# Keys of a sample group transposed in 32x32 blocks on VectorE, scores in 32x32 tiles of TensorE

## The chip, the cores and the metric

One core of one Trainium2 chip runs the whole program. The metric is the device time of one execution in microseconds; a kernel's time is the median of three runs. Times inside a profile are microseconds from the start of the profiled execution's span.

## The reference, cut to what matters

The program is one inference step of a two-layer decoder trunk, over 1024 prompt tokens and a sample group of 8 sequences with 8 new tokens each. The change touches the differential attention of the first layer, for the sample group: each sequence has 512 past keys in a paged cache (4 pages of 128 tokens, found by a page table), 8 heads, and two query/key components (c) of 64 channels per head, so a key of one token is 1024 numbers.

```python
q = rms_norm(zq.reshape(b, l, H_A, 2, DH_A), q_g) * (DH_A ** -0.5)
k = rms_norm(zk.reshape(b, l, H_A, 2, DH_A), k_g)
...
k_past = cache_k[j, page_table].reshape(db, past_len, H_A, 2, DH_A)
v_past = cache_v[j, page_table].reshape(db, past_len, H_A, DV_A)
k_all = jnp.concatenate([k_past, k], axis=1)
...
s = jnp.einsum('bqhcd,bkhcd->bhcqk', q, k)
s = s + bias                       # by the distance, the same for both components
s = jnp.where(causal, s, -jnp.inf)
p = jax.nn.softmax(s, axis=-1)
a = p[:, :, 0] - lam * p[:, :, 1]
return jnp.einsum('bhqk,bkhe->bqhe', a, v)
```

A sample has 8 heads x 2 components x 8 queries = 128 rows of scores over 512 past and 8 new keys. Everything here is float32.

## The kernel before

The program goes through stages: a projection of queries, keys and values with the attention of the prompt (to about 586 us), the stage of the sample group (about 586 to 832 us), and then the gated MLP, the output projection and the second layer. The change lies in the sample stage, with a little preparation ahead of it.

**The sample stage** walks over 32 pages, four for each of the 8 samples. Its loop over steps s (from L638 on) calls, in each step, the parts below with a lag of so many pages behind the page that is loaded. That table of lags, LAG = (10, 7, 5, 3) for out_t, av_s, att_t and soft, sets a rough order; a scheduler that orders the program when it is built then places each instruction on its engine's queue, and each engine takes its queue strictly in that order.

- pages (L517 to L522): a raw key page kp, 128 tokens x 1024 channels, 512 KB, is loaded on SP's queue. There are two kp buffers.
- vpages (L524 to L529): the same for a value page vp, six buffers, on SP as well.
- key_trans (L531 to L540): for each half of a page (hh = 0: heads 0 to 3, hh = 1: heads 4 to 7), TensorE transposes four 128x128 blocks into one PSUM bank (ktp, two banks, L539), and VectorE (hh = 0) or ScalarE (hh = 1) copies it into the transposed keys kT of that half (L540). There are three kT buffers, two to a sample.
- soft (L542 to L564): the scores ssc of a sample. The queries lie in qbd, for each head block-diagonal over its two components, with the rows of the other half zero. For each half and each of four column tiles of 32 columns there is one matmul with 128 channels and 512 past keys, and one with the 8 new keys (L550). VectorE then adds the bias to the last columns (L555), takes the maximum (snm, L558), ScalarE takes the exponential with its sum (spp, L560), and VectorE makes the reciprocal with its sign (sss, L561 and L562) and scales a combination matrix with it (cmb, L564).
- att_t (L567 to L577): matmuls with cmb transpose the probabilities and subtract the second component (an L571, ap L575), copied to sat by VectorE and ScalarE.
- av_s (L579 to L594): attention times values, sop (L586): four column tiles x four value pages and the new values; then squares on ScalarE (ssq), a norm on POOL, and son on VectorE (L593).
- out_t (L597 on): son is transposed (sot) and scaled to the output.

**The filling.** Between these steps the loop calls 52 units of projection work, about 4.8 to a sample, in a fixed order: first the rest of the gate units (gate_a, L242 to L259, PSUM name ga, 24 matmuls of up to 384 columns), then 36 units of the MLP's value branch (vb_unit, PSUM name zv, 24 matmuls of 256 columns). All take their accumulator from one PSUM name with two banks. A zv unit ends in a copy zs (L623), on VectorE for even and ScalarE for odd units, and a store on SP (L624).

**Ahead of the stage**, the prompt loop normalizes the sample rows' queries and keys and transposes them on TensorE per head (qk_trans with i == NT - 1), into qbd and ksT, and bias_sample loads the bias in 16 small DMAs.

## Time and profile before

| | |
|---|---|
| time, median of three runs | 1801.37 us (1799.54 to 1802.87) |
| span of the profiled execution (the page gives no other time of it) | 1806.1 us |
| TensorE: matmuls / weight loads | 1747.1 us (97%) / 1629.0 us (90%) |
| VectorE | 1012.4 us (56%) |
| ScalarE | 755.4 us (42%) |
| GpSimd (POOL) | 609.3 us (34%) |
| moved by DMA | 211.62 MB, mean 117 GB/s |

In the rows below PE is TensorE's matmuls, PEld its weight loads, DVE VectorE, ACT ScalarE, POOL GpSimd, SP SyncE, which only issues transfers (SPq). L12 is line 12 of the kernel. A busy share is an average over stages that have different limits, so a stage is read by stretches: how much of them an engine is busy, and, where it idles, which instruction or transfer ended the wait. "idle before <-X" is that time and what ended it. PEclk is the granted clock of TensorE as a share of full speed.

### The profile page before, as it was taken

The page shows a single profiled execution, that of the slowest core. Times are in us where ns is not written, and L with a number is a line of the kernel's source. Part 1 is how long each engine was busy: PE and PEld are TensorE (multiplying, and loading weights), DVE is VectorE, ACT ScalarE, POOL GpSimd, SP SyncE. Part 2 cuts the span into 40 slices and gives each one's busy share as a digit, 9 for nine tenths or more (in the row PEclk, how much of TensorE's full clock was granted, in tenths as well). Part 3 has the DMA queues.
Part 4 walks back from the last instruction along what each step waited for, and adds up shares of the span by engine and source line. Part 5 has one row for each costly group of instructions (what it writes and reads, how often), then busy time and mean ns, then how long its engine had stood idle before and what let it go on. Part 6 is the DMA issues. An engine that isn't in the chain of part 4 may idle for free.

```text
span 1806.1 us, 31855 instructions
## 1 busy us (share of the span) xinstructions
PE 1747.1 (97%) x11429; PEld 1629.0 (90%) x11429; DVE 1012.4 (56%) x2223; ACT 755.4 (42%) x1934; POOL 609.3 (34%) x893
## 2 busy tenths in 40 slices
PE   7999999999999899999899999999999999998999
PEld 6798999999999888889899999999999999996777
DVE  5898888988983233223832342444354455667442
ACT  4566656666664222223222232333343334345241
POOL 4555646655653221112721200044111232235230
PEclk8999999999999999999999999999999999999999
DMA  7102202211213766746221262432334244438741
GB/s 211 52 23 73 68 20 67 67 43 43 66 59 104 243 202 232 236 165 213 59 79 54 92 199 74 129 97 82 94 116 152 80 126 123 130 111 260 240 130 71
DMA packets 223302, 211.62 MB, mean 117 GB/s; under 512 B 22286, under 2 KB 201143, under 8 KB 223143
## 3 DMA queue, kind: packets, MB, share of 16 engines
q1 hardware_dynamic: 203510, 194.35, 34.7%
q10 hardware_dynamic: 19632, 15.21, 2.8%
q8 instruction: 91, 1.49, 0.4%
q14 instruction: 69, 0.56, 0.1%
HBM read 151.35 MB, written 56.24 MB: 115 GB/s over the span
## 4 chain that ended last, share of the span: by engine, by line
PE 62%; DVE 16%; DMA 9%; ACT 4%; POOL 4%; issue 4%; SPq 0%; ACTq 0%; POOLq 0%; DVEq 0%
PE o L1373 5%; PE yo L143 3%; PE yo L145 3%; PE yo L144 3%; PE vg L143 3%; PE vg L144 3%; PE vg L145 3%; DMA oT_d<-oTr 2%; DVE p L418 2%; PE zv L143 1%; PE zv L144 1%; PE zv L145 1%; PE o L434 1%; PE s L399 1%; PE qkv L143 1%
## 5 line engine op out<-in xcount | busy, mean ns | idle before, releaser
L412 ACT ACTIVATE p<-s,nm 128x256 f32<-128x256 f32 (+7 forms) x128 | 95.0, 747 | 38.3 <-DVE nm L409 22.3
L399 PE MATMUL s<-ks,qs 128*128 128x512 f32 (+3 forms) x384 | 96.5, 364 | 2.8 <-DVE ks L384 1.4
L87 ACT CAST qs<-qs 64x256 fp32r<-64x256 f32 x128 | 51.7, 404 | 76.8 <-DVE qs L381 74.2
L1120 POOL TENSOR_TENSOR e<-e,k 128x256 f32<-128x256 f32 (+1 forms) x50 | 42.4, 853 | 117.1 <-ACT e L1117 100.8
L338 POOL TENSOR_TENSOR sq<-qk 128x256 f32<-128x256 f32 (+1 forms) x72 | 46.9, 652 | 95.0 <-ACT qk L87 94.2
L434 PE MATMUL o<-v,at 128*128 128x128 f32 x576 | 76.8, 279 | 1.6 <-ACT at L87 1.6
L399 PEld LDWEIGHTS s<-ks,qs 128*128 128x128 f32 x384 | 64.9, 190 | 12.6 <-ACT p L412 2.8
L434 PEld LDWEIGHTS o<-v,at 128*128 128x128 f32 x576 | 71.4, 193 | 4.2 <-ACT at L87 2.6
L131 POOL TENSOR_TENSOR s<-s,mhalf 128x4 f32<-128x4 f32 (+1 forms) x72 | 73.3, 1018 | 5.3
L837 DVE TENSOR_TENSOR yp<-yp,yo 128x384 f32<-128x384 f32 (+1 forms) x48 | 25.3, 530 | 74.5 <-ACT yp L836 41.7
L407 DVE TENSOR_REDUCE nm<-s 128x1 f32<-128x640 f32 (+3 forms) x64 | 65.2, 1019 | 1.2
L747 POOL TENSOR_TENSOR u<-u,th 128x384 f32<-128x384 f32 (+1 forms) x24 | 28.7, 1194 | 99.9 <-DVE th L746 99.4
L405 DVE TENSOR_TENSOR s<-s,tb 128x256 f32<-128x256 f32 (+1 forms) x128 | 52.8, 412 | 8.9 <-PE s L399 5.6
L418 DVE SCALAR_TENSOR_TENSOR p<-p,fac,p 128x128 f32<-128x128 f32 (+3 forms) x64 | 55.1, 861 | 1.7
L1373 PE MATMUL o<-w1h,oh 128*128 128x512 f32 x128 | 53.0, 414 | 2.5 <-ACT oh L1350 2.5
L87 ACT COPY at<-atp 128x512 f32<-128x512 f32 (+2 forms) x96 | 44.5, 481 | 20.0 <-PE atp L427 19.8
L746 DVE SCALAR_TENSOR_TENSOR th<-th,gb 128x384 f32<-128x384 f32 (+1 forms) x24 | 12.6, 524 | 69.0 <-ACT th L745 69.0
L1373 PE MATMUL o<-w1l,oh 128*128 128x512 f32 x128 | 50.8, 397 | 0.0
L1373 PE MATMUL o<-w1h,ol 128*128 128x512 f32 x128 | 50.3, 407 | 0.0
L427 PE MATMUL atp<-cf,p 128*128 128x128 f32 x288 | 46.8, 275 | 1.9 <-DVE p L418 1.8
L343 POOL TENSOR_TENSOR qk<-qk,s 128x256 f32<-128x256 f32 (+1 forms) x72 | 46.6, 647 | 4.7
L381 DVE SCALAR_TENSOR_TENSOR qs<-qkt,qg,qs 64x128 fp32r<-64x128 f32 x128 | 44.5, 348 | 3.6
(825 smaller groups left out, 6340.4 us busy)
## 6 DMA issues: line engine op xcount, KB each, us to landing
kp<-in_cache_k SPq DMA_DIRECT2D x32, 512.0 KB
vp<-in_cache_v SPq DMA_DIRECT2D x32, 512.0 KB
or<-oT_d SPq DMA_DIRECT2D x16, 384.0 KB
vb_d<-zs SPq DMA_DIRECT2D x36, 128.0 KB
oT_d<-ob SPq DMA_DIRECT2D x8, 544.0 KB
gt<-g_d SPq DMA_DIRECT2D x34, 128.0 KB
xt<-in_x_prompt SPq DMA_DIRECT2D x8, 512.0 KB
out<-v ACTq DMA_DIRECT2D x64, 64.0 KB
```

Of the source, the lines that this page charges most:

```text
L87: act.activation(o, i_, AF.Copy, scale=scale) if scale is not None else act.copy(o, i_)
L131: pool.tensor_tensor(dst, dst, mhalf[:dst.shape[0], :n], ALU.pow)
L143: pe.matmul(out, lh, rh, start=(s == 0), stop=False)
L144: pe.matmul(out, lh, rl, start=False, stop=False)
L145: pe.matmul(out, ll, rh, start=False, stop=(s == n - 1))
L399: pe.matmul(sc[c][:, k0:k0 + w], qs[:, c, l], kts[h, j][:, c, :w], start=(l == 0), stop=(l == 1))
L405: dve.tensor_tensor(sc[c][:, lo:n], sc[c][:, lo:n], tb[:, h, 256 - (n - lo):], ALU.add)
L407: dve.tensor_reduce(nm[:, c:c + 1], sc[c][:, :n], axis=AX.X, op=ALU.max, negate=True)
L412: act.activation(pc[:, :n], sc[c][:, :n], AF.Exp, bias=nm[:, c:c + 1], accum_out=ss[:, c:c + 1])
L418: dve.scalar_tensor_tensor(pt[0][:, :n], pt[1][:, :n], fac, pt[0][:, :n], ALU.mult, ALU.add)
L434: pe.matmul(op[:, :P], at[:, j * P:(j + 1) * P], vts[h, j], start=(j == 0), stop=(j == i))
L1373: pe.matmul(it.mp[:r], lh[:, k, :r], rh[k][:, cs], start=(k == 0 and a == 0), stop=(k == KT - 1 and a == 2))
```

## The change

Queries and keys of the sample rows are no longer transposed on TensorE. Ahead of the stage, GpSimd multiplies the queries by the norm's weights (qgr), and queries and keys go to DRAM (qs_d, ks_d), two DMAs per head. The bias tile biasS gets the shape 128 x 4 x 34 and 32 small DMAs instead of 16. A mask qmask is added to the constants.

In the stage, the key order in the PSUM scores is by residue: of each page, tokens are cut into four groups a of 32, and each row group of TensorE works on one of them.

- key_trans: VectorE transposes each half page (128 x 512) in 32x32 blocks straight from kp into kT (now 128 x 16 x 130); neither TensorE nor PSUM takes part. GpSimd copies the sample's new keys (kn2, made once at the start of the stage) into the last two columns.
- q_rep (new, called behind key_trans of page 1 of each sample): one DMA of 512 KB brings the sample's 8 queries, 16 times over, into qx; GpSimd multiplies by the mask that leaves each row its own half and component; VectorE transposes 128 x 1024 in 32x32 blocks into qr, one buffer.
- soft: 128 matmuls with 32 channels, 32 columns of weights and 130 keys, each placed on one of the 16 tiles of 32x32 by tile_position, into four PSUM banks (in place of two, and the two of ktp). Bias and maximum go over the new shape; the exponential is cut in two, with two sums that VectorE adds.

The rest of the stage, its buffers (kp 2, vp 6, kT 3, two accumulator banks) and its lags are the same. The diff, cut to its core:

```diff
-        qbd = mid.tile([P, H, NB, 2, 2, 8], F32, name="qbd")
-        pool.memset(qbd, 0.0)
-        ksT = mid.tile([P, H, NS], F32, name="ksT")
         vsm = mid.tile([NS, H, P], F32, name="vsm")
-        biasS = mid.tile([P, 136], F32, name="biasS")
+        biasS = mid.tile([P, 4, 34], F32, name="biasS")
+        qgr = mid.tile([NS, P], F32, name="qgr")
+        qmask = mid.tile([P, 2 * H], F32, name="qmask")
...
-                nc.sync.dma_start(biasS[r0:r0 + 8, :], tb[0:8, h, 0:136])
+                nc.sync.dma_start(biasS[r0:r0 + 8, :, 0:32], tb[0:8, h, 0:128].rearrange("p (a k) -> p a k", a=4))
+                nc.sync.dma_start(biasS[r0:r0 + 8, :, 32:34], tb[0:8, h, 128:136].rearrange("p (a k) -> p a k", a=4))
...
+                if i == NT - 1:
+                    G[PRM['kg']].tensor_tensor(qk[:r, :128], qk[:r, :128], qgr, ALU.mult)
+                    nc.sync.dma_start(qs_d[:, h * P:(h + 1) * P], qk[:r, :128])
+                    nc.sync.dma_start(ks_d[:, h * P:(h + 1) * P], qk[:r, 128:])
+                    return None
...
-                if i == NT - 1:
-                    for c in range(2):
-                        q8 = slice(c * DH, (c + 1) * DH)
-                        act.activation(qbd[q8, h, :, h // 4, c, :], tp[q8, 0:NS].rearrange("p (b q) -> p b q", b=NB),
-                                       AF.Copy, scale=qg[q8])
-                    dve.tensor_copy(ksT[:, h, :], tp[:, 128:128 + NS])
-                    return None
...
+            kn = pb.tile([P, D], F32, tag="vn", name="kn", bufs=1)
+            dve.memset(kn, 0.0)
+            for a in range(4):
+                nc.sync.dma_start(kn[a * 32:a * 32 + 2 * NB, :],
+                                  ap_of(ks_d, 2 * a * D, [[8 * D, NB], [D, 2], [1, D]]))
+            knT = pb.tile([P, 32, 32], F32, tag="qx", name="knT", bufs=1)
+            dve.transpose(knT, kn.rearrange("p (j d) -> p j d", j=32))
+            kn2 = pb.tile([P, NB, 32, 2], F32, name="kn2")
+            pool.tensor_copy(kn2, knT[:, :, :2 * NB].rearrange("p j (b e) -> p b j e", b=NB))
+            qrs = {}
+
+            def q_rep(b):
+                qx = pb.tile([P, D], F32, tag="qx", name=f"qx{b}", bufs=1)
+                nc.sync.dma_start(qx, ap_of(qs_d, b * 8 * D, [[0, 16], [D, 8], [1, D]]))
+                q3 = qx.rearrange("p (n d) -> p n d", d=DH)
+                pool.tensor_tensor(q3, q3, qmask[:, :, None].broadcast_to([P, 2 * H, DH]), ALU.mult)
+                qr = pb.tile([P, 32, 32], F32, tag="qr", name=f"qr{b}", bufs=1)
+                dve.transpose(qr, qx.rearrange("p (j d) -> p j d", j=32))
+                qrs[b] = qr
+
             def key_trans(b, g):
                 kp = kps.pop((b, g))
                 if g == 0:
-                    kTs[b] = [pb.tile([P, 4, 512], F32, tag="kT", name=f"kT{b}_{hh}", bufs=3) for hh in range(2)]
+                    kTs[b] = [pb.tile([P, 16, 130], F32, tag="kT", name=f"kT{b}_{hh}", bufs=3) for hh in range(2)]
+                    for hh in range(2):
+                        pool.tensor_copy(kTs[b][hh][:, :, P:], kn2[:, b, hh * 16:hh * 16 + 16, :])
                 for hh in range(2):
-                    tp = psb.tile([P, 512], F32, tag="kt", name=f"ktp{b}_{g}_{hh}", bufs=2)
-                    for q in range(4):
-                        h = hh * 4 + q
-                        pe.transpose(tp[:, q * P:(q + 1) * P], kp[:, h * P:(h + 1) * P], ident)
-                    (act.copy if hh else dve.tensor_copy)(kTs[b][hh][:, :, g * P:(g + 1) * P], tp.rearrange("p (h k) -> p h k", h=4))
+                    dve.transpose(kTs[b][hh][:, :, g * 32:(g + 1) * 32],
+                                  kp[:, hh * 512:(hh + 1) * 512].rearrange("p (j d) -> p j d", j=16))
 
             def soft(b):
                 kT = kTs.pop(b)
-                st = psb.tile([P, 1024], F32, tag="ss", name=f"ssc{b}", bufs=1)
-                for cols in (slice(0, 512), slice(512, 520)):
-                    for hh in range(2):
+                qr = qrs.pop(b)
+                st = psb.tile([P, 4, 512], F32, tag="ss", name=f"ssc{b}", bufs=1)
+                for hh in range(2):
+                    for q in range(4):
                         for g in range(4):
-                            h = hh * 4 + g
-                            rhs = kT[hh][:, g, :] if cols.start == 0 else ksT[:, h, b * 8:(b + 1) * 8]
-                            pe.matmul(st[g * 32:(g + 1) * 32, cols], qbd[:, h, b].rearrange("p x c q -> p (x c q)"), rhs,
-                                      start=(hh == 0), stop=(hh == 1))
+                            for a in range(4):
+                                ar = slice(a * 32, (a + 1) * 32)
+                                pe.matmul(st[g * 32:(g + 1) * 32, a, :130], qr[ar, (hh * 4 + g) * 4 + q, :], kT[hh][ar, g * 4 + q, :],
+                                          start=(hh == 0 and q == 0), stop=(hh == 1 and q == 3), tile_position=(a * 32, g * 32))
                 vn = pb.tile([8, D], F32, tag="vn", name=f"vn{b}", bufs=1)
                 nc.scalar.dma_start(vn, vsm[b * 8:(b + 1) * 8].rearrange("p h d -> p (h d)"))
                 vps[b, NPG] = vn
-                dve.tensor_tensor(st[:, 384:520], st[:, 384:520], biasS, ALU.add)
+                dve.tensor_tensor(st[:, :, 96:130], st[:, :, 96:130], biasS, ALU.add)
                 nm = pb.tile([P, 1], F32, tag="snm", name=f"snm{b}", bufs=2)
                 ss = pb.tile([P, 1], F32, tag="sss", name=f"sss{b}", bufs=2)
-                dve.tensor_reduce(nm, st[:, :520], axis=AX.X, op=ALU.max, negate=True)
+                s2 = pb.tile([P, 2], F32, tag="ss2", name=f"ss2{b}", bufs=2)
+                dve.tensor_reduce(nm, st[:, :, :130], axis=AX.XY, op=ALU.max, negate=True)
                 pp = pb.tile([P, 520], F32, tag="spp", name=f"spp{b}", bufs=2)
-                act.activation(pp, st[:, :520], AF.Exp, bias=nm, accum_out=ss)
+                act.activation(pp[:, 0:512].rearrange("p (g a k) -> p a g k", g=4, a=4),
+                               st[:, :, 0:P].rearrange("p a (g k) -> p a g k", g=4), AF.Exp, bias=nm, accum_out=s2[:, 0:1])
+                act.activation(pp[:, 512:520].rearrange("p (a e) -> p a e", a=4), st[:, :, P:130], AF.Exp, bias=nm, accum_out=s2[:, 1:2])
+                dve.tensor_tensor(ss, s2[:, 0:1], s2[:, 1:2], ALU.add)
...
                     key_trans(b, g)
+                    if g == 1:
+                        q_rep(b)
...
+    row = np.arange(P) % 32
+    for h in range(H):
+        for c in range(2):
+            cf[:, 326 + h * 2 + c] = np.where((row // 16 == h // 4) & (row // 8 % 2 == c), DH ** -0.5, 0.0)
```

Three places show what the scheduler makes of it. In the rows a trailing number of a name is a running number of its buffer; kT_0 and kT_1 are the key halves of heads 0 to 3 and 4 to 7, ktp_g_hh the PSUM transposes and kp_g the raw page g, ssc the scores of a sample, snm their maximum, sss the sum and scale, son the output of the sample before, zs_i and zv_i projection unit i.

VectorE before, around the softmax of the fourth sample:

```order
L555 TENSOR_TENSOR ssc_9492<-ssc_9492,biasS 128x136
L593 TENSOR_TENSOR son_9484<-sop_9463,sms_9486 128x256
L558 TENSOR_REDUCE snm_9512<-ssc_9492 128x1
L561 RECIPROCAL sss_9513<-sss_9513 128x1
L562 TENSOR_TENSOR sss_9513<-sss_9513,csgn 128x1
L564 TENSOR_SCALAR cmb_9519<-cf,sss_9513 128x128
L540 COPY kT_0_9399<-ktp_1_0_9521 128x4x128
L623 COPY zs_6_9580<-zv_6_9555 128x256
L540 COPY kT_0_9399<-ktp_2_0_9583 128x4x128
```

Bias, maximum and softmax stand together, with the copies of pages 1 and 2 of the next sample behind them.

VectorE in the changed kernel, at the same place:

```order
L560 STREAM_TRANSPOSE kT_0_9617<-kp_2_9864 128x16x32
L560 STREAM_TRANSPOSE kT_1_9618<-kp_2_9864 128x16x32
L560 STREAM_TRANSPOSE kT_0_9617<-kp_3_9916 128x16x32
L560 STREAM_TRANSPOSE kT_1_9618<-kp_3_9916 128x16x32
L577 TENSOR_TENSOR ssc_9702<-ssc_9702,biasS 128x4x34
L550 STREAM_TRANSPOSE qr_9851<-qx_9848 128x1024
L560 STREAM_TRANSPOSE kT_0_10090<-kp_0_10046 128x16x32
L581 TENSOR_REDUCE snm_9834<-ssc_9702 128x1
L586 TENSOR_TENSOR sss_9835<-ss_9836 128x1
L587 RECIPROCAL sss_9835<-sss_9835 128x1
L588 TENSOR_TENSOR sss_9835<-sss_9835,csgn 128x1
L649 COPY zs_6_9900<-zv_6_9875 128x256
```

Now the transposes of pages 2 and 3 stand ahead of the bias (those of pages 0 and 1 in rows before these), a query tile and page 0 of the sample after next ahead of the maximum, and the zs copy behind all of them.

ScalarE before, at the same sample:

```order
L591 ACTIVATE ssq_9485,sms_9486<-sop_9463 128x128
L540 COPY kT_1_9400<-ktp_0_1_9407 128x4x128
L560 ACTIVATE spp_9515,sss_9513<-ssc_9492,snm_9512 128x520
L540 COPY kT_1_9400<-ktp_1_1_9527 128x4x128
L540 COPY kT_1_9400<-ktp_2_1_9589 128x4x128
L623 COPY zs_7_9642<-zv_7_9617 128x256
```

The exponential stands behind the copy of page 0 and ahead of those of pages 1 and 2.

ScalarE in the changed kernel:

```order
L617 ACTIVATE ssq_9695,sms_9696<-sop_9673 128x128
L583 ACTIVATE spp_9838,ss_9836<-ssc_9702,snm_9834 128x4x4x32
L585 ACTIVATE spp_9838,ss_9836<-ssc_9702,snm_9834 128x8
L649 COPY zs_7_9952<-zv_7_9927 128x256
```

ScalarE loses its copies of kT_1; its zs copy of unit 7 stands right behind the two exponentials, which take the maximum.

## Rows read from the trace of the kernel before

**Rows 1.** Engine totals of the page: busy time, share of span, instructions.
```profile
PE 1747.1 (97%) x11429; PEld 1629.0 (90%) x11429; DVE 1012.4 (56%) x2223; ACT 755.4 (42%) x1934; POOL 609.3 (34%) x893
```

**Rows 2.** Window: us; busy of PE, PEld, DVE, ACT, POOL; PEclk; DMA share; GB/s.
```profile
674.13:768.53 94.40, 91.92 (x909) 79.19 (x912) 29.02 (x63) 27.04 (x77) 9.72 (x16) 1.00 0.68 228
```

**Rows 3.** Chain that ended last, 586 to 831: start, us, engine, operation.
```profile
674.13 1.04 PE sop L586 x16
...
675.74 6.50 DMA kp<-in_cache_k
...
686.54 0.87 PE ktp L539 x8
...
747.68 1.04 PE sop L586 x16
...
749.27 5.93 DMA kp<-in_cache_k
```

**Rows 4.** Groups, 586 to 832: count, busy, mean ns, idle before and its releasers.
```profile
L539 PE MATMUL ktp<-cf,kp 128*128 128x128 f32 x256 | 34.5, 274 | 8.2 <-ACT kT L540 4.7 <-DMA kp<-in_cache_k 2.5 <-DVE kT L540 1.0
...
L540 DVE COPY kT<-ktp 128x512 f32<-128x512 f32 x32 | 22.0, 689 | 32.9 <-PE ktp L539 32.8
...
L623 DVE COPY zs<-zv 128x256 f32<-128x256 f32 x19 | 8.0, 422 | 40.4 <-PE zv L145 40.2
```

**Rows 5.** Timeline of PE, then PEld, one sample's sop and scores: start, us, engine.
```profile
649.38 1.93 PE L586 MATMUL sop<-vp,sat 128*32 128x256 f32 x32
...
651.81 1.92 PE L550 MATMUL ssc<-kT,qbd 128*32 128x512 f32 x16
653.55 0.29 PE L550 MATMUL ssc<-ksT,qbd 128*32 128x8 f32 x16
653.77 0.45 PE L143 MATMUL ga<-xh,wg7h 128*128 128x384 f32 x1
...
652.27 0.13 PEld L550 LDWEIGHTS ssc<-kT,qbd 128*32 128x32 f32 x4 [0.30 <-issue]
652.70 0.13 PEld L550 LDWEIGHTS ssc<-kT,qbd 128*32 128x32 f32 x4 [0.30 <-issue]
```

**Rows 6.** Timeline of VectorE, then ScalarE, one sample's softmax.
```profile
678.62 0.31 DVE L555 TENSOR_TENSOR ssc<-ssc,biasS 128x136 f32<-128x136 f32 x1 [4.02 <-PE ssc L550]
678.96 0.70 DVE L558 TENSOR_REDUCE snm<-ssc 128x1 f32<-128x520 f32 x1
...
680.77 0.16 DVE L562 TENSOR_TENSOR sss<-sss,csgn 128x1 f32<-128x1 f32 x1
680.96 0.29 DVE L564 TENSOR_SCALAR cmb<-cf,sss 128x128 f32<-128x128 f32 x1
...
679.75 0.70 ACT L560 ACTIVATE spp<-ssc,snm 128x520 f32<-128x520 f32 x1 [1.27 <-DVE snm L558]
```

**Rows 7.** Timeline of SP's queue: start, us to issue, line, transfer.
```profile
675.20 0.35 SPq L528 DMA_DIRECT2D vp<-in_cache_v  x1
...
687.65 0.34 SPq L521 DMA_DIRECT2D kp<-in_cache_k  x1
```

**Rows 8.** Windows behind that last issue, columns as in rows 2.
```profile
687.65:692.00 4.35, 4.35 (x38) 4.00 (x37) 0.34 (x2) 1.04 (x3) 0.00 (x0) 1.00 0.80 253
692.00:695.00 3.00, 3.00 (x28) 3.00 (x26) 0.69 (x1) 0.89 (x2) 0.00 (x0) 1.00 0.01 3
```

**Rows 9.** Timeline of PE: successive matmuls of a zv unit, then of a gate unit.
```profile
829.74 0.28 PE L143 MATMUL zv<-wv3h,xh 128*128 128x256 f32 x1
829.86 0.28 PE L144 MATMUL zv<-wv3l,xh 128*128 128x256 f32 x1
...
639.85 0.33 PE L144 MATMUL ga<-xl,wg6h 128*128 128x384 f32 x1
640.02 0.33 PE L145 MATMUL ga<-xh,wg6l 128*128 128x384 f32 x1
```

**Rows 10.** Windows at a later stall of TensorE, columns as in rows 2.
```profile
885.62:888.25 2.63, 0.00 (x0) 0.00 (x0) 2.63 (x3) 0.44 (x1) 2.63 (x2) 1.00 0.00 0
888.25:891.67 3.42, 3.14 (x10) 3.14 (x11) 2.75 (x5) 0.40 (x1) 3.25 (x5) 0.50 0.21 58
```

More of the change, by code (lines that the diff above doesn't have):

```diff
@@ L105, in hybrid_step @@
     v_d = dram.tile([T, D], F32, name="v_d")
+    qs_d = dram.tile([NS, D], F32, name="qs_d")
+    ks_d = dram.tile([NS, D], F32, name="ks_d")
     g_d = dram.tile([T, D], F32, name="g_d")
@@ L274, in small_consts @@
                 nc.sync.dma_start(kg, k_norm_g.rearrange("o c d -> o (c d)").broadcast_to([P, P]))
+                nc.sync.dma_start(qmask, c_f32[:, 326:342])
+                nc.sync.dma_start(qgr, q_norm_g.rearrange("o c d -> o (c d)").broadcast_to([NS, P]))
                 nc.sync.dma_start(qg, q_norm_g.rearrange("o c d -> (o c d)")[:, None])
@@ L296, in xprep @@
                     nc.scalar.dma_start(gbc, norm0_g.broadcast_to([P, D]))
-                    nc.sync.dma_start(cf, c_f32)
+                    nc.sync.dma_start(cf, c_f32[:, 0:326])
                 xn = pa.tile([P, D], F32, tag="at", name=f"xn{i}", bufs=PRM["atb"])
@@ L1439, in _constants @@
 def _constants():
-    cf = np.zeros((P, 326), np.float32)
+    cf = np.zeros((P, 342), np.float32)
     cf[:, 0:P] = np.eye(P)
```

## The prediction, made before the changed kernel ran

> **What bounds the kernel now.** Read first the engine totals: TensorE is busy for 97% of the span [rows 1], so work taken off it can count. Then go to the stretch that the change touches, the sample stage from about 586 to 832 us. In the middle of it TensorE is busy for 91.92 of 94.40 us, VectorE for 29.02, at full clock [rows 2]: a stage bound by TensorE, with VectorE two thirds idle. The chain of waits gives its beat: the attention-times-values matmuls (sop) of one sample start at 674.13, those of the third sample after it at 747.68, so a sample takes 24.5 us [rows 3]. The groups show what the change removes: 256 key transposes on TensorE, before which it idled 8.2 us in all, and the copies behind them [rows 4]. A group of eight runs in 0.87 us [rows 3].
>
> **What is removed.** 32 pages x 0.87 = 27.8 us of TensorE [rows 3], and the 8.2 us in front of them [rows 4]: -36 us. ScalarE loses its copies and VectorE's copies (0.689 us) become transposes; in the averages neither is short of time. The 16 transposes of sample queries and keys before the stage are under 2 us by the same price and are counted at nothing.
>
> **The score matmuls.** A sample's scores were eight matmuls of 512 columns on four column tiles, each in two passes, and eight short ones of 8 columns. The 16 long passes go four at a time: the weights of one round load 0.43 us after those of the last (652.27, 652.70), and the next work starts at 653.77, 1.96 us after 651.81 [rows 5]. The changed kernel issues 128 matmuls of 130 columns, two passes each as before, 16 per tile. A pass is 130/512 x 0.43 = 0.11 us; if all 16 tiles run at once that is 16 x 0.11 = 1.75 us. The 16 short passes took 0.22 us, 14 ns each [rows 5]; at that issue pace 256 take 3.6 us. I take 2.0 us, no change, as the four-tile rows come out at their array time, and keep 3.6 (+13 us over eight samples) for the range. The rows also show the passes of neighbouring tiles starting together though a matmul's own second pass lies between them in the program. The Trainium skill (TensorE: Matmul & The Clock Gate, Step-by-step: what each phase is for) says that matmuls stay in program order and only weight loads are pulled ahead. By that rule a tile would wait for its neighbour's second pass and scores would cost 128 x 0.11 = 14 us a sample; the four-tile rows speak against it, and it stays as a rival.
>
> **What is moved, and why I expect a loss.** The price that decides is the new order on VectorE, not the work. Before, a page reached VectorE only through TensorE, and between two copies stood the softmax and the drains. Now VectorE waits for the page itself. In the changed order, all the next sample's pages 1 to 3 (and after them its query tile and page 0 of the sample after) stand ahead of this sample's maximum. Behind the maximum stand the softmax, and behind that the copies that free TensorE's two accumulators: VectorE's zs copy, and ScalarE's, which stands behind the exponential. Only two raw page buffers exist, so pages 2 and 3 cannot start to load until pages 0 and 1 are transposed, and the second half of page 0 must wait for the first half of this sample's scores, which frees its key tile. So three loads in a row lie between the scores and the maximum, with nothing but two units of projection on TensorE to cover them.
>
> Clock it from the start of one sample's sop (time 0), for samples 2 to 6, where the units are zv:
> - TensorE: sop and scores end at 4.4 (649.38 to 653.77) [rows 5]. Two units of 24 matmuls, 0.12 us apart [rows 9], are 5.8: at 10.2 it needs a drained accumulator.
> - The value load needs the buffer of sop's first block, free after a quarter of 1.93 us [rows 5], 0.5; the page-1 load follows it by about 0.54 us (675.20 [rows 7] to 675.74 [rows 3]), so at 1.1. Loads issued in such a burst landed after 6.50 and 5.93 us [rows 3]; one issued at 687.65 had landed by 692.00, the DMA engines then standing idle: at most 4.4 us [rows 7, 8]. I take 5.5 for bursts and 4.4 for the last, which has one load beside it. Page 1 is there at 6.6.
> - A transpose of 128x512 does not occur in the trace; the copy of the same shape takes 0.69 us [rows 4]. I take that, with bounds of half and double. Three transposes: 8.7; page 0's buffer is free at 8.0.
> - Page 2 lands at 13.5, is transposed by 14.9; page 3, issued at 9.1, lands at 14.6, done 16.3.
> - Bias 0.31 [rows 6] and the query tile (twice 0.69): 17.9. Page 0 of the sample after was issued when page 2 was transposed (14.9), lands at 19.3: 20.0.
> - Maximum 0.70, exponential 0.70 plus a short second one and its sums (1.3 together), four small steps of about 0.16 to 0.3 [rows 6], zs copy 0.42 [rows 4]: 23.3.
> TensorE idles from 10.2 to 23.3: **13.1 us**, five times: 65.5 us. Sample 1 is followed by two gate units of 24 x 0.173 = 4.2 us [rows 9] and then by a matmul that needs the softmax scale: idle from 12.8 to 22.8, 10 us. Sample 0 has only two loads in this place, one issued early, before its maximum: about 4.5 us. Sample 7 has no page behind it.
>
> After a stall the clock counts too. TensorE did nothing from 885.62 to 888.25, and from 888.25 to 891.67 its granted clock was 0.50, that is 1.2 GHz [rows 10]. 3.4 us at half pace lose 1.7 us; six long stalls: +10 us. The bounds are 0 and 3.4 us each (one stretch more).
>
> Other additions are covered: the query replication (one more 512 KB load a sample and a GpSimd multiply of 1024 columns) is done a sample ahead; the small copies of new keys go to GpSimd; the split bias loads come early, on SP, where nothing waits for them until the first scores. If the query load were late, the same VectorE queue would wait for it, so it would add to the stall, not make another.
>
> **Sum** against the profiled execution, whose span is 1806.1 us: -36 + 65.5 + 10 + 4.5 + 10 = +54, so 1860. The median of the runs shown, 1801.4, is 4.7 us under that span (the page gives no other time of that execution): **1855 us**.
>
> **Range.** Cheap end: every load 4.3 us gives a zs copy at 21.2, idle 11.0; with transposes at half the copy's time idle is about 8, and without clock loss the sum is -36 + 40 + 5 + 1 = +10: 1811. Dear end: loads at 6.4 give idle 16.9 and 13.8; 85 + 14 + 8, clock 20, -36: +91, and the score matmuls at issue pace 13 more: 1905.
>
> **Rivals.**
> 1. *It gains: the pages are there in time.* If the loads of pages 2, 3 and 0 landed so early that the zs copy came before 10.2, only the removal would be left: 1801.4 - 36 = about 1766. It decides at a load time: with loads of 2.5 us my clock still gives a zs copy at 18.1, so both loads and transposes would have to be far quicker than any row. For it speaks only that VectorE's total is small. Chance 0.07.
> 2. *Score passes start strictly in order.* Scores take 14 us a sample; the VectorE chain is then partly hidden under them (the first half ends 6.9 us after the scores start). With the same loads the zs copy comes at about 25, TensorE reaches its wait at 22, idle 3.3: -36 + 8 x 11.8 + 6 x 3.3 = +78, 1880, inside the range. Against it: the four-tile rows. Chance 0.08.
> 3. *Tiles do not overlap at all*, loads included: 256 passes at 0.11 us are 28 us a sample, +26 x 8 - 36 = +172, 1975. Chance 0.03.
> 4. *The stall exists but pays just the gain*, at the cheap end or below (loads near 3 us once fewer values are in flight): within 3.6 us of 1801. Chance 0.03.
> My forecast has 0.79.
>
> **How the numbers follow.** About 0.2% (3.6 us) is what a measurement can tell from no change. Faster: rival 1, 0.07. Same: rival 4, 0.03. Slower: the forecast and rivals 2 and 3, 0.90. Rivals 1, 3 and 4 are left outside the range with a small tail of the forecast.
>
> **What would show it.** In the profile after: key transposes gone from TensorE, 64 stream transposes of about 0.7 us on VectorE; scores still about 2 us a sample; VectorE idle on DMA kp several us at a time; TensorE with a gap of some 13 us once a sample, two units after the scores, ended by VectorE or ScalarE (zs or cmb), and a granted clock below 1 behind the gaps; samples some 33 to 35 us apart. Wrong would be: samples about 21 us apart with TensorE full (rival 1), or scores of 14 us or more with little idle (rivals 2, 3).

## The result and the profile after

| | before | after |
|---|---|---|
| time, median of 4 runs | 1800.53 us (1799.54 to 1802.87) | 1864.74 us (1863.33 to 1866.95) |
| ratio | | 1.0349, interval 1.0332 to 1.0366 |
| span of the profiled execution | 1806.1 us | 1864.1 us (that execution: 1865.78) |

The change costs 64 us. The engine totals of the changed kernel, which answer to [rows 1]:

```profile
PE 1750.5 (94%) x12949; PEld 1639.0 (88%) x12949; DVE 1039.1 (56%) x2265; ACT 736.3 (40%) x1902; POOL 633.3 (34%) x925
```

TensorE's busy time did not fall, although 256 transposes are gone; its share did. Windows of the sample stage, from 586 us to the last zv matmul, of the kernel before and then of the changed one, and three samples of it (sop to sop; columns as in [rows 2]):

```profile
586.00:831.90 245.90, 237.60 (x2108) 209.25 (x2107) 68.49 (x146) 63.27 (x175) 37.16 (x56) 1.00 0.62 205
```
```profile
586.00:894.50 308.50, 245.28 (x3619) 220.25 (x3618) 96.62 (x192) 48.05 (x157) 53.68 (x79) 0.89 0.54 175
685.27:787.60 102.33, 78.02 (x1277) 70.08 (x1276) 31.18 (x63) 13.86 (x48) 12.71 (x19) 0.85 0.51 173
```

The stage grew by 62.6 us between these marks. A mark that moves with the program is better: from the start of the last matmul of the prompt's attention (570.3 before, 566.3 after) to the start of the last zv matmul it is 261.6 and 328.3 us, 66.7 more. The program ahead of the first mark and behind the second is nearly the same in every kernel of this document, and still its time scatters: over the 14 traces the first mark lies at 564.6 to 570.3 us, and what follows the second takes 966.1 to 976.5 (974.2 before, 969.6 after). So the profiled execution of before is a long one, and the spans differ by only 58.0 us.

TensorE's idle time in the stage rose from 8.3 to 63.2 us, and the granted clock fell from 1.00 to 0.89. A sample takes 34.1 us (102.33 / 3) where it took 24.5 [rows 3].

One sample, from its sop at 685.27. VectorE's timeline (times before "DVE" are start and length):

```profile
690.11 0.42 DVE L619 TENSOR_TENSOR son<-sop,sms 128x256 f32<-128x256 f32 x1 [4.31 <-POOL sms L133]
691.83 1.90 DVE L560 STREAM_TRANSPOSE kT<-kp 128x512 f32<-128x512 f32 x3 [1.30 <-DMA kp<-in_cache_k]
696.49 1.31 DVE L560 STREAM_TRANSPOSE kT<-kp 128x512 f32<-128x512 f32 x2 [2.76 <-DMA kp<-in_cache_k]
701.12 1.31 DVE L560 STREAM_TRANSPOSE kT<-kp 128x512 f32<-128x512 f32 x2 [3.33 <-DMA kp<-in_cache_k]
702.35 0.28 DVE L577 TENSOR_TENSOR ssc<-ssc,biasS 128x136 f32<-128x136 f32 x1
702.54 1.22 DVE L550 STREAM_TRANSPOSE qr<-qx 128x1024 f32<-128x1024 f32 x1
703.68 0.70 DVE L560 STREAM_TRANSPOSE kT<-kp 128x512 f32<-128x512 f32 x1
704.30 0.66 DVE L581 TENSOR_REDUCE snm<-ssc 128x1 f32<-128x520 f32 x1
```

TensorE and ScalarE in the same sample:

```profile
685.27 1.93 PE L612 MATMUL sop<-vp,sat 128*32 128x256 f32 x32
...
687.59 2.59 PE L572 MATMUL ssc<-kT,qr 32*32 32x130 f32 x157
693.63 1.79 PE L572 MATMUL ssc<-kT,qr 32*32 32x130 f32 x81 [3.45 <-issue]
...
702.09 0.28 PE L147 MATMUL zv<-wv0h,xl 128*128 128x256 f32 x1
706.40 0.58 PE L145 MATMUL zv<-wv0h,xh 128*128 128x256 f32 x1 [4.04 <-ACT zs L649]
...
705.06 0.69 ACT L583 ACTIVATE spp<-ssc,snm 128x512 f32<-128x512 f32 x1 [16.05 <-DVE snm L581]
...
705.98 0.37 ACT L649 COPY zs<-zv 128x256 f32<-128x256 f32 x1
```

The scores end at 695.4, but their bias is added at 702.35 and their maximum taken at 704.30: before each of the three groups of transposes VectorE stands at a page load. ScalarE waits 16 us for that maximum with the zs copy behind it, and TensorE, after two units, waits for the zs copy. A second thing was not in the prediction: TensorE stops for 3.45 us inside the scores, and the profile shows nothing that it waits for ("issue").

What TensorE waited for in the stage (us in all, times, longest), and the groups of the new work:

```profile
PE ssc L572 <- issue: 22.2, 7, 4.3
PE an L597 <- DVE cmb L590: 13.2, 4, 6.5
PE zv L152 <- DVE zs L649: 6.1, 1, 6.1
PE ga L145 <- DVE g L256: 5.1, 3, 2.4
PE zv L145 <- ACT zs L649: 4.0, 1, 4.0
```
```profile
L560 DVE STREAM_TRANSPOSE kT<-kp 128x512 f32<-128x512 f32 x64 | 41.8, 690 | 56.1 <-DMA kp<-in_cache_k 56.1
L572 PE MATMUL ssc<-kT,qr 32*32 32x130 f32 x2048 | 38.0, 295 | 26.0 <-issue 22.2 <-ACT spp L585 3.7
```

VectorE waited 56.1 us for pages ahead of its transposes, and its cmb, its zs and the gates' g stand on the same queue as those waits.

**What the 'issue' stalls are.** The trace also records the transfers that bring instructions. Set beside the stops inside a sample's scores or just behind them, from matmul start to matmul start (worked out from the trace's records, one line per stop; not a view of the profile):

```
stop (us)          length   an instruction packet of 16 KB landed   TensorE went on after
617.07 to 619.46    2.39    618.19                                  1.27 us
656.65 to 660.96    4.31    659.55                                  1.41
689.91 to 693.63    3.72    692.28                                  1.35
725.46 to 728.78    3.32    727.40                                  1.38
758.64 to 763.17    4.53    761.86                                  1.31
792.29 to 796.85    4.56    795.38                                  1.47
827.57 to 829.26    1.69    827.76                                  1.50
858.26 to 861.17    2.91    859.89                                  1.28
```

Eight of eight stops, 27.4 us in all, end 1.3 to 1.5 us after such a packet. They come after different numbers of score passes (238, 195, 175, then behind all 256, 221, 176, 131, 222), so no one operand explains them. The same step, 1.2 to 1.5 us from a packet's landing to the next pass, ends all six 'issue' stops inside the scores of e1_order and all six of e5_offload below. A sample's scores are 256 passes, each with a weight load, in about 4 us. Seven of the eight packets took 0.9 to 1.0 us from start to landing, so it is their start that comes late (up to 2.2 us after the stop has begun); what sets it is not shown.

### The profile page after: what moved, and what is told of

Same layout as the page of the kernel before. It is cut to its first block, busy times and chain, and to the rows that moved or that the text cites. A ratio compares the mean times of both kernels' runs of the same rounds, so it can differ in the third digit from the quotient of the medians.

```text
span 1864.1 us, 35001 instructions
## 1 busy us (share of the span) xinstructions
PE 1750.5 (94%) x12949; PEld 1639.0 (88%) x12949; DVE 1039.1 (56%) x2265; ACT 736.3 (40%) x1902; POOL 633.3 (34%) x925
## 5 line engine op out<-in xcount | busy, mean ns | idle before, releaser
L401 PEld LDWEIGHTS s<-ks,qs 128*128 128x128 f32 x384 | 64.2, 189 | 10.9 <-ACT p L414 3.6
L560 DVE STREAM_TRANSPOSE kT<-kp 128x512 f32<-128x512 f32 x64 | 41.8, 690 | 56.1 <-DMA kp<-in_cache_k 56.1
L572 PE MATMUL ssc<-kT,qr 32*32 32x130 f32 x2048 | 38.0, 295 | 26.0 <-issue 22.2
L572 PEld LDWEIGHTS ssc<-kT,qr 32*32 32x32 f32 x2048 | 29.2, 106 | 31.2 <-issue 28.9
```

What stands on the lines that cost most here:

```text
L401: pe.matmul(sc[c][:, k0:k0 + w], qs[:, c, l], kts[h, j][:, c, :w], start=(l == 0), stop=(l == 1))
L572: pe.matmul(st[g * 32:(g + 1) * 32, a, :130], qr[ar, (hh * 4 + g) * 4 + q, :], kT[hh][ar, g * 4 + q, :], start=(hh == 0 and q == 0), stop= ...
```

## The experiments

Theory A is the prediction's: VectorE's order puts page waits ahead of the softmax, and TensorE waits for what stands behind. The rival B puts the loss on the stops inside the scores, C says that waits behind VectorE only move. On the same chip the kernel before took 1797.2 us beside e1 to e4, 1808.3 beside e5 to e7, 1796.6 beside e8 to e10, 1798.9 beside e11 and a median of 1802.0 (1797.4 to 1809.2, 8 runs) beside e12. The experiments but e12 are single executions, so a difference of some us between two times tells little, least of all across these groups. The stage from mark to mark, as in the section above, leaves out the scatter ahead of it and behind it:

| kernel | time, us | the kernel before beside it | stage, mark to mark, us |
|---|---|---|---|
| before | 1800.5 | | 261.6 |
| changed | 1864.7 | 1800.5 | 328.3 |
| e1_order | 1827.8 | 1797.2 | 290.9 |
| e2_kp3 | 1854.4 | 1797.2 | 313.3 |
| e3_order_half | 1807.8 | 1797.2 | 262.1 |
| e4_order_split | 1825.0 | 1797.2 | 286.6 |
| e5_offload | 1827.1 | 1808.3 | 294.3 |
| e6_offload_split | 1824.8 | 1808.3 | 283.9 |
| e7_all | 1833.5 | 1808.3 | 295.9 |
| e8_removed | 1772.9 | 1796.6 | 234.9 |
| e9_offload_oT | 1817.1 | 1796.6 | 280.1 |
| e10_kp3_oT | 1823.9 | 1796.6 | 280.9 |
| e11_later_scores | 1826.4 | 1798.9 | 288.9 |
| e12_two_steps | 1814.3 | 1802.0 | 276.2 |

Where the text below gives a stage's length without more, it is counted from 586 us.

**e1_order.** In the changed kernel, with cmbs[b] = cmb kept in soft. Each tiny copy reads the cmb of an earlier sample and writes into the tile that a transpose fills next, so the transpose cannot come ahead of that sample's softmax:

```diff
+                if b - 1 in cmbs:
+                    dve.tensor_copy(qr[0:1, 0, 0:1], cmbs[b - 1][0:1, 0:1])
...
+                last = cmbs.get(b - 1, cmbs.get(b - 2))
                 for hh in range(2):
+                    if g < 2 and last is not None:
+                        n = 32 if g == 0 else 96
+                        dve.tensor_copy(kTs[b][hh][0:1, 0, g * 32:g * 32 + n], last[0:1, 0:n])
                     dve.transpose(...)
```

> The transposes of the next sample's pages 1 to 3, the query tile and page 0 of the sample after are put behind this sample's softmax on VectorE, by tiny copies out of cmb into the tiles that they write; nothing else is changed. Theory A (VectorE waits for page loads ahead of the softmax, and TensorE waits for what stands behind): the gap of some 10 to 13 us a sample goes; what is left is the removal (-36), scores of 4.2 instead of 2.0 us (+18) and the stalls inside the scores that the trace of the changed kernel puts down to 'issue' (22 to 27 us): about 1810, range 1800 to 1830. Theory B (the stalls inside the scores set the beat and the order costs nothing): 1855 to 1870. Theory C (the wait only moves, now to the zs copies that stand between the transposes): 1835 to 1855.

Measured: 1827.78 us. VectorE in one sample of it:

```profile
691.78 0.31 DVE L583 TENSOR_TENSOR ssc<-ssc,biasS 128x136 f32<-128x136 f32 x1 [4.31 <-PE ssc L578]
692.12 0.70 DVE L587 TENSOR_REDUCE snm<-ssc 128x1 f32<-128x520 f32 x1
...
695.28 1.88 DVE L566 STREAM_TRANSPOSE kT<-kp 128x512 f32<-128x512 f32 x3
...
700.83 1.30 DVE L566 STREAM_TRANSPOSE kT<-kp 128x512 f32<-128x512 f32 x2 [1.64 <-DMA kp<-in_cache_k]
```

The bias now waits for the scores, not for pages, and 37 us of the 64 are back (the stage from mark to mark is as much shorter), by order alone: same work, some tiny copies more. Beside its own run of before it is still 30.6 us dearer. B alone (1855 or more) falls. It lies at the dear end of A's range, 18 us above its figure, and just under C's: 8.4 us of waits for g, 3.3 for zs and 3.1 for the weights' low halves are left, all behind VectorE, so some of what C says is true too.

**e2_kp3.** kp 3 buffers, spp and sat one each, VectorE's order left.

> Three raw page buffers instead of two (room made by one buffer for spp and sat), with the VectorE order of the changed kernel. Theory A: the chain of loads between scores and softmax is one load shorter (4.4 to 5.5 us), so samples 1 to 6 gain about that each: 26 to 33 us, 1832 to 1840. Theory B (stalls inside the scores set the beat): 1858 to 1868.

Measured: 1854.36 us, 10 less than the change, not 26 to 33, and under the range of theory B too. The loads' issue on SP (first fence) and VectorE (second), in a sample whose sop starts at 713.4:

```profile
700.34 13.88 SPq L650 DMA_DIRECT2D vb_d<-zs  x5
714.47 0.34 SPq L530 DMA_DIRECT2D vp<-in_cache_v  x1
715.01 0.34 SPq L523 DMA_DIRECT2D kp<-in_cache_k  x1
715.60 1.15 SPq L530 DMA_DIRECT2D vp<-in_cache_v  x1
716.93 0.53 SPq L523 DMA_DIRECT2D kp<-in_cache_k  x1
```
```profile
720.26 0.71 DVE L560 STREAM_TRANSPOSE kT<-kp 128x512 f32<-128x512 f32 x1 [1.77 <-DMA kp<-in_cache_k]
723.15 2.49 DVE L560 STREAM_TRANSPOSE kT<-kp 128x512 f32<-128x512 f32 x4 [2.17 <-DMA kp<-in_cache_k]
729.37 1.31 DVE L560 STREAM_TRANSPOSE kT<-kp 128x512 f32<-128x512 f32 x2 [3.73 <-DMA kp<-in_cache_k]
...
732.52 0.66 DVE L581 TENSOR_REDUCE snm<-ssc 128x1 f32<-128x520 f32 x1
```

The key loads stand on SP's queue behind value loads, which go out only once sop has freed their buffers, and both stand behind five stores of zs, each waiting for its copy, the last issued at 713.91. So a third buffer lets two loads go together but not earlier. From sop to the maximum it is 19.1 us here (713.4 to 732.52) and 19.0 in the changed kernel (685.27 to 704.30). What was gained lies elsewhere: sop to sop is 29.9 and 30.5 us in two of the last samples, where the changed kernel has 32.3 and 33.2; which wait gave it was not separated.

**e3_order_half.** e1_order with `for q in range(2)`: half of the channel blocks of every head are left out of the scores.

> As e1_order, but the scores leave out half of their channel blocks: 64 matmuls a sample instead of 128, on half of the channels of each head. Theory A with scores bound by the number of their instructions: the scores take 2.1 instead of 4.2 us and no longer run dry of instructions: e1_order minus 17, and minus most of the 22 to 27 us of stalls: 1770 to 1785. If the stalls inside the scores are waits for data and not for instructions: only the 17 us go, about 1793.

Measured: 1807.79 us, 20 less than e1_order, neither 1770 to 1785 nor 1793. The scores start 2.1 us apart from first to last, half of before, and no stop is left in them. The stage itself is 29.4 us shorter than e1_order's, 17 from TensorE's busy time (237.81 to 220.73) and 12 from its idle time; the part behind it is 9 longer, within its scatter. So the second branch's 17 us are right, and most of the stalls do go as the first said, although waits for g rose from 8.4 to 12.3 us. With half of the scores the stage is back at the length of before (262.1 and 261.6 from mark to mark).

**e4_order_split.** e1_order with the scores in two parts:

```diff
+                b, g = at(2)
+                if g == NPG - 1:
+                    score(b, 0)
```

> As e1_order, but the first half of a sample's scores (heads 0 to 3) is issued one step earlier, so that projection work lies between the halves; all the work is done. If TensorE runs dry of instructions inside the scores (512 of them in some 4 us), the slow work between the halves lets the next instructions come in: e1_order minus 10 to 25 us. If the stalls have another cause (data, or the pace of issue), the same as e1_order within 4 us.

Measured: 1825.02 us, 3 less than e1_order (4.3 in the stage from mark to mark). TensorE's waits in e1_order, then in e4_order_split:

```profile
PE ssc L578 <- issue: 13.7, 6, 3.5
PE ga L145 <- DVE g L256: 8.4, 3, 3.2
PE zv L147 <- issue: 4.5, 2, 4.1
```
```profile
PE ga L145 <- DVE g L256: 10.1, 5, 2.9
PE an L611 <- DVE cmb L603: 3.6, 3, 1.5
PE zv L145 <- ACT wv1h L176: 3.6, 1, 3.6
PE zv L146 <- DVE wv2l L177: 2.9, 1, 2.9
PE ssc L580 <- issue: 2.3, 1, 2.3
```

The stops fall from 18.2 to 2.3 us with the same instructions spread over more time, which agrees with the packets above: it is the density of instructions. But the time hardly moves, since other waits take their place and the clock gives no more (0.95 and 0.94 in the stage). By its time alone the run falls to the branch 'another cause'; the waits show that the stops are real, and that taking them away is worth little alone.

**e5_offload, e6_offload_split, e7_all.** From e1_order: all zs copies and stores to ScalarE, the low halves of the weights (of the gates too, from head 3 on) to GpSimd; with kp 3 (e5), with the split and kp 2 (e6), and with kp 3, the split and the gates' product on ScalarE and GpSimd (e7):

```diff
-                (act.copy if i % 2 else dve.tensor_copy)(zs, mp[:, :256])
-                nc.sync.dma_start(vb_d[...], zs)
+                act.copy(zs, mp[:, :256])
+                nc.scalar.dma_start(vb_d[...], zs)
...
-                    wv[c] = load_w(..., f"wv{c}")
+                    wv[c] = load_w(..., f"wv{c}", 1)
```

> e1_order, and besides what stood behind page waits on VectorE goes to other engines: all zs copies and their stores to ScalarE and its queue, the low halves of the sample stage's weights to GpSimd; three page buffers (one for spp and sat). The gates' product (g) stays on VectorE. Theory C (after e1_order TensorE still waits for small work that stands behind page waits on VectorE): the waits for zs and for the weights' low halves go, some 8 us, and the third buffer gives a little: 1812 to 1822. Theory D (the rest of e1_order's loss is all in the stalls inside the scores and the clock behind them): 1825 to 1830.

> As e5_offload with two page buffers, and the scores issued in two halves with projection work between, as in e4_order_split. Theory C+fetch (both the waits behind VectorE and the instruction stalls cost, and each was filled by the other before): e1_order minus 8 minus 15: 1800 to 1810. If the split costs as much as it saves: 1815 to 1825.

> As e6_offload_split, with three page buffers and the gates' product moved from VectorE to ScalarE (copy out of PSUM) and GpSimd (sum and product): nothing that TensorE's accumulators wait for is left behind a page wait. Theory C+fetch: the gates' waits (10 us in e4_order_split) go as well: 1788 to 1800. If the pages themselves are late by then (the loads' rate), the scores wait for kT and it stays at 1805 or more.

Measured: 1827.07, 1824.82 and 1833.48 us, beside 1808.27 of before. In e5 no wait for zs or low halves is left, yet 'issue' stands at 22.0 us in the scores (13.7 in e1_order): time freed at one wait was spent at the next. In e6 the stops are under 2 us; late keys (5.2), the gates (9.7) and a clock of 0.92 in the stage take it back. In e7 the gates wait for ScalarE instead (10.0 us), and the scores for the query tile (4.3). The gains that theory C forecast fail in all three: e5 falls in theory D's range, e6 in that of a split that costs as much as it saves, e7 above 1805. The times are not to be set against e1_order's, since before was 11 us slower beside them; from mark to mark e5's stage is 3.4 us longer than e1_order's, e6's 2.7 shorter than e4_order_split's and e7's 12.0 longer than e6's. Waits do move.

**e8_removed.** The kernel before, without TensorE's transposes (keys are copied as they lie, not transposed):

```diff
-                    tp = psb.tile([P, 512], F32, tag="kt", name=f"ktp{b}_{g}_{hh}", bufs=2)
-                    for q in range(4):
-                        h = hh * 4 + q
-                        pe.transpose(tp[:, q * P:(q + 1) * P], kp[:, h * P:(h + 1) * P], ident)
+                    tp = kp[:, hh * 512:(hh + 1) * 512]
```

> The kernel before with TensorE's key transposes left out: VectorE and ScalarE copy each half page straight from the raw page (so the keys are not transposed; scores, queries and everything else as before). It shows what the removal is worth alone, with copies that wait for the pages themselves. If the removal is worth its work and waits (36 us): 1762 to 1770. If pages that VectorE and ScalarE wait for take it back even with the old scores, as theory A has it where the order puts them ahead of other work: 1775 to 1800.

Measured: 1772.90 us beside 1796.59, 24 less. Its stage, and VectorE around one softmax:

```profile
586.00:801.00 215.00, 210.54 (x1828) 178.80 (x1827) 59.21 (x143) 64.31 (x173) 35.95 (x54) 1.00 0.67 229
```
```profile
663.10 0.30 DVE L552 TENSOR_TENSOR ssc<-ssc,biasS 128x136 f32<-128x136 f32 x1
664.61 0.43 DVE L537 COPY kT<-kp 128x512 f32<-128x512 f32 x1 [1.22 <-DMA kp<-in_cache_k]
664.96 0.69 DVE L555 TENSOR_REDUCE snm<-ssc 128x1 f32<-128x520 f32 x1
...
667.71 0.43 DVE L537 COPY kT<-kp 128x512 f32<-128x512 f32 x1 [0.47 <-DMA kp<-in_cache_k]
```

The stage is 30.9 us shorter than before (26.7 from mark to mark), TensorE idles 4.5 us in it, at full clock, although VectorE waits 48.8 us for pages, nearly as long as in the changed kernel (56.1), and ScalarE 37.5. In this program's order on VectorE one page copy stands between bias and maximum in three of the eight samples and none in the other five. So the removal does pay, and page waits cost little where the order keeps the softmax ahead of them. The run also lacks the query tile and the new scores, so it does not give the price of the order by itself; e1_order does.

**e9_offload_oT, e10_kp3_oT.** e6_offload_split with oTr 4 and g2 2 buffers (spp, sat 1); e10 with kp 3, oTr 3, g2 1.

> e6_offload_split with four buffers for the gate's oTr and two for g (one for spp and sat), since there ScalarE's exponentials and tanh stood behind a load of oTr that waited for an earlier store (5.8 us at 656.66). If these waits were what the gates and the softmax of samples 0 to 2 wait for: e6_offload_split minus 8 to 12, 1810 to 1817. If other waits take their place: within 4 us of 1825.

> As e9_offload_oT with three page buffers and three of oTr, one of g. The waits for late kT (5.2 us in e6_offload_split) go as well: 1805 to 1815; if the third page buffer is of no more use than in e2_kp3: 1812 to 1820.

Measured: 1817.09 and 1823.85 us. e9 is 8 under e6_offload_split, but before was 12 faster beside it; the stage is 6.7 us shorter from 586 us and 3.8 from mark to mark, so the forecast of 8 to 12 is not shown to have held. The waits for g fell from 9.7 to 5.8 us. In e10 the stage has the length of e9's (280.9 and 280.1) and the 7 us more lie behind it, in the scatter: the third page buffer again brings nothing, and waits for late keys stay at 5.1.

**e11_later_scores, e12_two_steps.** e9_offload_oT with the scores one step later, then with all behind them one more (what e12 has otherwise stands behind a #):

```diff
-LAG = (10, 7, 5, 3)
-VL = 3
+LAG = (11, 8, 6, 4)    # e12: (12, 9, 7, 4)
+VL = 4                 # e12: 5
...
-                    if g < 2 and last is not None:
+                    if g in (0, 2) and last is not None:
...
-                    if g == 1:
+                    if g == 2:                                   # e12
                         q_rep(b)
...
-                pool.tensor_tensor(q3, q3, qmask...
+                dve.tensor_tensor(q3, q3, qmask...               # e12
```

> e9_offload_oT with the scores, the softmax and all behind them one step (one page) later, so that on VectorE only pages 2 and 3 stand behind the softmax of the sample before, and a sample's keys are complete before its scores come up on TensorE. If e9_offload_oT's waits for late kT (4.0 us) and the slow clock around them (18.8 us of the stage lost to the half clock, in part while idle) are what keeps it from the kernel before: 1798 to 1808. If the stage is held by the scores' 4.2 us a sample and the gates, 1812 to 1818.

> e11_later_scores with the probabilities' transposition and all behind it one step later still, the query tile behind the softmax as well, and its mask multiply on VectorE, so that GpSimd (low halves of the weights) waits for no load. In e11_later_scores TensorE waited 10.6 us for cmb and 9.9 us for GpSimd's low halves: if these go and nothing takes their place: 1798 to 1808, at the kernel before or some us above. If the waits move again, as they did in e7_all and e11_later_scores: 1815 to 1830.

Measured: 1826.42 us, then 1814.32 us (5 runs, 1811.72 to 1815.25), ratio to before 1.0062, interval 1.0031 to 1.0092. In e11 the waits for late keys went (0.2 us left) and those for cmb (10.6) and for GpSimd's low halves (9.9) came, and it lies above both of its ranges. In e12 the low halves' waits went and cmb fell to 5.5, but 6.2 us behind son and 4.8 for a weight's high half came: the waits moved again, and the time lies just under the range given for that. Its stage:

```profile
586.00:845.50 259.50, 235.10 (x3636) 206.71 (x3635) 94.07 (x195) 54.92 (x178) 56.55 (x92) 0.95 0.64 211
```

It is the fastest complete version with the new scores that ran, 0.6% slower than the kernel before, which no complete version beat. Beside e8's stage (215.00), which has the old scores, TensorE is busy for 25 us more and idle for 20 more. Whether a better order would win was not settled.

## Why the prediction was right, step by step

The forecast of 1855 (1811 to 1905), slower, held: 1864.7. By its own steps:

- **What is removed (-36).** The work was sized rightly: in e8 TensorE is busy for 27.1 us less in the stage, where 27.8 were taken. Of the 8.2 us of waits only 3.8 go, since others come. The run is 24 us faster and the stage 26.7 shorter from mark to mark (30.9 from 586 us), so the term is some 10 us too high.
- **The order on VectorE.** Right in mechanism and, for a sample, within 2.4 us at every step. Counted from sop, predicted and measured (685.27 as zero): three transposes done 8.7 / 8.5, page 2 done 14.9 / 12.5, page 3 done 16.3 / 17.2, query tile done 17.9 / 18.5, page 0 of the sample after 20.0 / 19.1, TensorE back at work 23.3 / 21.1. A transpose was taken at 0.69 us from the copy of that shape; it takes 0.690. Samples were said to be 33 to 35 us apart; sop to sop they are 33.7, 34.5, 34.1, 32.3 and 33.2 from the second sample on. e1_order, which changes the order only, gives 37 us back.
- **TensorE's idle time (13.1 us a sample).** The beat was right, its filling not. In the sample above TensorE should have run out of work at 10.2 and does so at 16.9 (two units, the last matmul at 702.09): the scores stop for 3.7 us and take 2.0 longer than taken, and the units take 1.0 longer, at half clock in part. Idle at the zs copy are then 4.2 us. That is 10.9 in all, up to 21.1. So the sign that was named, one gap of some 13 us a sample, did not appear. VectorE sets the beat and all of it lies under that one cover, which is why the sum came near although some of its terms did not: in the stage idle time was to rise by 72 us and busy time to fall by 18, and they rose by 54.9 and 7.7.
- **The score matmuls (2.0 us, "no change").** Mis-sized: the term that failed. Undisturbed they take 4.15 us from first to last start (720.89 to 725.04), 16 ns a pass: the bound of 3.6 us at issue pace was the better reading, and the array time the wrong choice. 2.2 us x 8 = 17 us, hidden in the changed kernel under VectorE's beat, and read in e3_order_half, where half of the passes take 17 us of busy time away.

The rows that decide that term, an undisturbed sample's scores (after the first 18 passes) and, in e3_order_half, half of them:

```profile
721.31 4.00 PE L572 MATMUL ssc<-kT,qr 32*32 32x130 f32 x238
```
```profile
651.53 1.90 PE L578 MATMUL ssc<-kT,qr 32*32 32x130 f32 x110
```

The Trainium skill (TensorEngine Tiling (Array Packing), Instruction Overhead) puts the overhead of each matmul at about 60 cycles; at 2.4 GHz that would be 25 ns a pass and 6.4 us for 256, an estimate from that page. The trace shows 16 ns, less than that.

- **Rival 2 (passes strictly in order, 14 us).** Excluded by its price: 4.15 us; so is rival 3 (28 us). Rivals 1 and 4 fall with the time and with samples 34 us apart. The Trainium skill (TensorE: Matmul & The Clock Gate, Step-by-step: what each phase is for) says that matmuls stay in program order. As rival 2 read it, with the two passes of a matmul next to each other in the program and the second waiting for the first, it does not fit the 4.15 us; but no record here names the tile of a pass or the order in the program, so the rule itself is neither shown nor refuted.
- **Stops for instructions.** Not foreseen: 27.4 us in the changed kernel, inside or just behind the scores. They lie under VectorE's cover there; with the order mended (e1) they are 18.2 us of TensorE's 35.1 idle.
- **The clock (10 us).** Low, by an estimate. The stage has 64.8 us at a granted clock of 0.50 (1.2 GHz), in 13 stretches, TensorE busy for 53.9 of them. A unit that ran wholly behind a gap took 5.2 us (706.40 to 711.62) where one at full clock takes 2.9. From the stage: busy time +7.7, transposes -27.8 to -34.5 (the group's own busy time [rows 4]), scores +17 leaves some 18 to 25 us, at most 0.44 x 53.9 = 24 by the pace of that unit; so about 18 to 24.
- **Sum and median.** The medians differ by 64.2 us where the terms gave 54, so the sum is 10 short, and the stage from mark to mark (+66.7) holds all of it; the spans differ by 58.0 only because the profiled execution of before was a long one. The five samples that were clocked are not where it is short: by the starts of sop their intervals are 46.7 us longer than before's in sum, where the terms give 51 (13.1 idle - 4.5 removed + 1.7 clock, each). The first interval is 13.1 us longer (7 by the terms, 10 - 4.5 + 1.7), and the last 8.3, where the terms give 4.5 less; units of projection fall differently on the two, so no single term is shown to be the cause. That errors of both signs left so little is in part luck.
- **Side results.** Redone, the clock of the prediction gives a zs copy at 20.8 instead of 21.2 with all loads at 4.3 us, and at about 16 instead of 18.1 with loads of 2.5. Neither changes the range or the verdict on rival 1.

## What to carry to other kernels

Before work is moved to an engine that is idle on average, read what it will wait for and what stands behind it on its queue: this change cost 64 us, and some 30 with the same transposes behind the softmax. Many small tiled matmuls can be priced by their number and not by their columns: here a pass took 14 ns with 8 columns [rows 5] and 16 ns with 130. In a dense run of them TensorE can stand waiting for its next instructions. When several waits lie under one cover, each of them taken away alone gives little: compare the idle time, the clock and the waits of the stage, not the one wait. And where the parts that a change does not touch scatter by several us, compare the stage from mark to mark, not the total.

## What the hardware showed that was not expected

TensorE stopped 1.7 to 4.6 us within dense runs of small matmuls and went on 1.3 to 1.5 us after a 16 KB instruction packet had landed, eight times of eight; splitting the run in two took most of the stops away (18.2 to 2.3 us). Passes on 16 tiles started every 16 ns at full clock, while by the pace of the four-tile rows one takes some 0.11 us (an estimate, 130/512 x 0.43), so several ran at once. A stretch at a granted clock of 0.50 (1.2 GHz) began within 0.9 us of the end of six of the eight stops above (660.11, 694.24, 728.37, 762.50, 796.64, 861.49). In the row below, which holds the gap that ended at 706.40, the unit behind it takes 5.2 us instead of 2.9.

```profile
704.48:711.30 6.82, 4.90 (x23) 4.90 (x24) 1.59 (x6) 1.29 (x5) 1.90 (x1) 0.50 0.42 115
```
